# Three unused tiles among the constants of a one-layer decoder kernel

## The chip, the core and the metric

The kernel runs on one core of one Trainium2 chip. The time is device microseconds of one execution, given as the median of three runs. The trace used below is one profiled execution of the same program. Five engines matter: TensorE (PE, its weight loads are listed as PEld), VectorE (DVE), ScalarE (ACT), GpSimd (POOL) and SyncE (SP), which issues nearly all DMAs.

## The reference: what is computed

One decoder layer over 1024 tokens of width 1024, in float32. In short:

```python
h = rms_norm(x, norm_mix)
proj = h @ w_in                       # q, k, v of three mixers, and gates
oa = diff_attention(...)              # A: 4 heads, two softmaxes each
ob = banded_attention(..., 128, sink) # B: 8 heads, window 128
oc = nsa_attention(...)               # C: compressed + selected + window 512
y = einsum('nbsm,nmd->bsnd', [oa, ob, oc], w_branch)
x = x + sum(sigmoid(mg) * y) @ w_out
h = rms_norm(x, norm_mlp)
x = x + square(relu(h @ w_up)) @ w_down
```

## The kernel before

**Arithmetic.** Every float32 operand of a matrix product is split into a high and a low part by `split` (lines 87 to 91): ACT copies it to the 32-bit matmul type (the high part, line 90), and POOL or DVE subtracts that from the source (the low part, line 91). `mm3` (lines 115 to 120) then issues three matmuls into one bank of PSUM: high by high (line 118), high by low (119 or 120), low by high. In the profile a matmul reads `out<-moving,stationary`: the moving operand is streamed through the array, up to 512 columns of it, and the stationary one, 128 columns, is put in first by a weight load (PEld). A stationary slice is thus 128 float32, that is 512 bytes of each partition, and all slices of a tile lie at steps of 512 bytes.

**Stages, in order of time.** `run` (line 174) goes through them:

- Normalisation of the input into `hh` and `hl` (high and low part of the transposed, normalised input, pool `hT`), projections of mixer A and B (`project`, line 494: moving the weights, 384 or 396 columns wide, stationary `hh`/`hl`), compression, attention A and B: to 590 us.
- Mixer C, in two groups `g`: `project_c` (512 columns of weights moving, stationary `hh`/`hl`; 590 to 621 us and about 883 to 960 us), then attention C mixed on PE with `gates` (line 1095: moving `hh`/`hl`, 512 columns, stationary weights `wh`/`wl`) and, for the second group, with `first_branch` (line 1141: moving and stationary both from pool `wp`). `mix` (line 155) lays a generator of dense matmuls between the fine steps of the attention, by costs written into the code; the order on PE is the program's order, and gates are the filler that covers the attention's softmax on DVE and ACT. To 1216 us.
- `merge_and_mlp` (line 1159): the other two branch products (moving `ob` or `oc`, stationary weights that come in turn from the pools `pre` and `wx`, line 107; 1216 to 1311 us); the output projection (lines 1309 to 1318: moving `wo`, stationary `mh`/`ml`; 1311 to 1410 us).
- The MLP, as seven half-size products per pair of feature tiles, 16 pairs. Up (`up_pair`, line 1356: moving `mh`/`ml` or the sums `th`, stationary weights from `pre` and `main`; 1410 to 1736 us): each pair has 7 x 4 x 3 = 84 matmuls. Down (lines 1474 to 1519: moving weights, stationary the activations, both from `pre` and `main`; 1736 us to the end), also 84 a pair.

**Memory.** SBUF is filled from both ends by two stacks of pools. The left stack begins at byte 384 of each partition (256 bytes of DMA scratch and four constants of 32 bytes are below it). The right one ends at byte 229,344, which is 480 modulo 512. A tile's size is rounded up to 32 bytes. At the bottom of the left stack lie `cst` (`ident` 512 bytes, `nhalf` 32) and `ca` (`identr`, `gk`, `gsw`, five small ones, `cgate`, then `kct` and `vct`, 1024 bytes each). Everything else on the left begins where these two end; `ca` is released at 1216 us, so that the later pools begin where `cst` ends. From the built program, the addresses modulo 512 at which the matmul operands lie before the change ("residue" from here on; all slices of one tile share it):

| operand | pool, side | residue before |
|---|---|---|
| `hh`, `hl` | `hT`, right | 480 |
| weights, mixers A and B (396 float32 wide) | `wp`, left | 320, 384, 448, 0, 64 ... in steps of 64 |
| states of A and B | `s0`, `s1`, left | 320 |
| weights and `first_branch` operands, mixer C | `wp`, left | 192 |
| states of mixer C (base) | `sp`, left | 192 |
| `ph`, `pl` (transposed probabilities) | `at`, right | 160, and 480 in mixer C |
| `ob`; `oc` of the first half | `bb`, `br`, right | 480 |
| `oc` of the second half | `bl`, left | 416 |
| branch weights, in turn | `pre`, right; `wx`, left | 480; 416 |
| `wo` | `wo0`, `wo1`, right | 480 |
| `mh`, `ml`; `th` | `mp`, `tf`, left | 416 |
| MLP weights, activations of the down product | `pre`, `main`, right | 480 |

Of the kernel before, what the change touches and what calls it, by code (L numbers as in the profile page):

```python
# [11 lines left out]
F32 = mybir.dt.float32  # L12
# [5 lines left out]
P = 128  # L18
# [57 lines left out]
class Kernel:  # L76
# [238 lines left out]

    def idents(self):
        nc = self.nc
        self.ident = self.cst.tile([P, P], F32, name="ident")
        make_identity(nc, self.ident)
        self.identr = self.ca.tile([P, P], F32R, name="identr")  # L320
        nc.vector.tensor_copy(self.identr, self.ident)
        self.nhalf = self.cst.tile([P, 8], F32, name="nhalf")
        nc.vector.memset(self.nhalf, -0.5)
        self.gk = self.ca.tile([P, 3, HD], F32, name="gk")
        self.gsw = self.ca.tile([P, 2, HD], F32, name="gsw")

    def constants(self, tmp):
        nc, a, c = self.nc, self.a, self.ca
        ld = nc.sync.dma_start

        gains = tmp.tile([P, 8, HD], F32, name="gains")
        ld(gains, a["qk_gain"].broadcast_to([P, 8, HD]))
        stt = nc.vector.scalar_tensor_tensor
        stt(self.gk[:, 0, :], gains[:, 0, :], -0.125, gains[:, 1, :], op0=ALU.mult, op1=ALU.mult)
        stt(self.gk[:, 1, :], gains[:, 2, :], -0.125, gains[:, 3, :], op0=ALU.mult, op1=ALU.mult)
        stt(self.gk[:, 2, :], gains[:, 4, :], -0.125, gains[:, 5, :], op0=ALU.mult, op1=ALU.mult)
        stt(self.gsw[:, 0, :], gains[:, 4, :], -0.125, gains[:, 6, :], op0=ALU.mult, op1=ALU.mult)
        stt(self.gsw[:, 1, :], gains[:, 4, :], -0.125, gains[:, 7, :], op0=ALU.mult, op1=ALU.mult)

        dl = tmp.tile([P, 4, HD], F32, name="dl")  # L340
        ld(dl, a["diff_lambda"].broadcast_to([P, 4, HD]))
        pr = tmp.tile([P, 2, HD], F32, name="pr")
        nc.vector.tensor_tensor(pr, dl[:, 0:4:2, :], dl[:, 1:4:2, :], op=ALU.mult)
        ls = tmp.tile([P, 4], F32, name="ls")
        nc.vector.tensor_reduce(ls[:, 0:2], pr, axis=AX.X, op=ALU.add)
        nc.scalar.activation(ls[:, 2:4], ls[:, 0:2], AF.Exp)
        self.nlam = c.tile([P, 1], F32, name="nlam")
        stt(self.nlam, ls[:, 3:4], -LAM_INIT, ls[:, 2:3], op0=ALU.add, op1=ALU.subtract)
        self.subln = c.tile([P, 1], F32, name="subln")
        ld(self.subln, a["diff_subln"])  # L350
        nc.vector.tensor_scalar(self.subln, self.subln, 1.0 - LAM_INIT, None, op0=ALU.mult)
        self.sink = c.tile([P, 2, 8], F32, name="sink")
        ld(self.sink[:, 0, :], a["sinks"].broadcast_to([P, 8]))
        nc.vector.tensor_scalar(self.sink[:, 1, :], self.sink[:, 0, :], -1.0, None, op0=ALU.mult)
        self.wmask = c.tile([P, P], F32, name="wmask")
        ld(self.wmask, a["c_wmask"])
        self.cval = c.tile([P, 1], F32, name="cval")
        ld(self.cval, a["c_cval"])
        self.pos = c.tile([P, 2, 16], F32, name="pos")
        ld(self.pos, a["cmp_pos"])  # L360
        self.cgate = c.tile([P, NT, 24], F32, name="cgate")

        self.kct = c.tile([P, 2, P], F32R, name="kct")
        self.vct = c.tile([64, 2, P], F32R, name="vct")

# [1216 lines left out]
```

## Time and profile before

| | us |
|---|---|
| median of 3 runs | 2076.6 |
| lowest, highest | 2073.64, 2076.71 |
| span of the profiled execution | 2073.6 |

The profiled execution's span is the lowest run's time, so nothing lies around it. In the views below, a group of instructions is written as line, engine, operation, tiles, shape and count, then its busy time, the mean duration of one in ns, and the idle time before it with the engine that ended it. A view by windows gives, for each stretch of time, how long each engine was busy and (in brackets) how many of its instructions reach into the stretch, and the granted clock of TensorE as a share of full speed (PEclk).

### The profile page before, as it was taken

How to read it: one execution, taken by the hardware profiler on the slowest of the kernel's cores; microseconds unless marked ns; L12 is line 12 of the kernel's file. 1: busy time of each engine (PE TensorE's matmuls, PEld its weight loads, DVE VectorE, ACT ScalarE, POOL GpSimd, SP SyncE). 2: the span in 40 equal slices, each digit the busy share in tenths (PEclk: the TensorE clock that was granted, in tenths of full speed). 3: DMA queues.
4: the chain of work that ended last, by engine and by line, in shares of the span. 5: the costliest groups of instructions: out<-in, count | busy, mean ns of one | idle time of the engine just before them, and what ended most of it. 6: DMA issues, size and time to landing. Idle time of an engine off the chain costs nothing. (4 is left out here: it accounts for less than half of the span.)

```text
span 2073.6 us, 30616 instructions
## 1 busy us (share of the span) xinstructions
PE 1950.6 (94%) x9806; PEld 1615.6 (78%) x9806; DVE 1420.5 (69%) x3231; ACT 1019.3 (49%) x2626; POOL 948.4 (46%) x1137
## 2 busy tenths in 40 slices
PE   7999998998899999999999899999899998999998
PEld 7777777788688788787888677787688886888876
DVE  6757677788838767648676745657755444889898
ACT  5456555566636555536555533325445544434331
POOL 4555345354252212152221327217444444789784
PEclk9999999999999999999999899999999999999998
DMA  6131012011201111202142556425544346345343
GB/s 216 50 102 52 3 55 58 14 50 37 85 24 64 54 53 50 71 30 93 61 151 64 168 180 208 153 89 159 173 163 155 138 143 249 121 158 168 122 142 112
DMA packets 122557, 219.47 MB, mean 106 GB/s; under 512 B 14420, under 2 KB 35412, under 8 KB 122396
## 3 DMA queue, kind: packets, MB, share of 16 engines
q1 hardware_dynamic: 120812, 211.75, 31.3%
q10 hardware_dynamic: 1584, 5.77, 0.8%
q8 instruction: 77, 1.26, 0.3%
q14 instruction: 84, 0.69, 0.1%
HBM read 156.59 MB, written 64.81 MB: 107 GB/s over the span
## 5 line engine op out<-in xcount | busy, mean ns | idle before, releaser
L91 POOL TENSOR_TENSOR wl<-wr,wh 128x512 fp32r<-128x512 f32 (+3 forms) x246 | 326.1, 1332 | 282.1 <-ACT wh L90 236.8
L90 ACT ACTIVATE wh<-wr 128x512 fp32r<-128x512 f32 (+3 forms) x258 | 150.4, 591 | 182.3 <-PE mm L119 122.5
L705 PE MATMUL sc<-st 128*128 128x256 f32 (+5 forms) x736 | 201.6, 356 | 15.4 <-ACT p L737 15.0
L90 ACT ACTIVATE ph<-tr 128x384 fp32r<-128x384 f32 (+3 forms) x280 | 138.3, 496 | 118.0 <-PE tr L753 97.1
L91 DVE TENSOR_TENSOR pl<-tr,ph 128x384 fp32r<-128x384 f32 (+3 forms) x280 | 155.3, 558 | 45.7 <-ACT ph L90 42.4
L750 POOL MEMSET ph<- 128x128 f32 x152 | 34.7, 228 | 301.2 <-PE ac L895 256.6
L705 PEld LDWEIGHTS sc<-st 128*128 128x128 f32 x736 | 126.3, 192 | 55.7 <-ACT p L737 23.4
L118 PE MATMUL mm<-hh,wh 128*128 128x512 f32 x384 | 160.0, 417 | 0.0
L120 PE MATMUL mm<-hh,wl 128*128 128x512 f32 x384 | 152.5, 397 | 0.0
L119 PE MATMUL mm<-hl,wh 128*128 128x512 f32 x384 | 152.4, 397 | 0.0
L119 PE MATMUL mm<-wl,wh 128*128 128x512 f32 x352 | 140.4, 399 | 9.4 <-POOL wl L91 9.4
L118 PE MATMUL mm<-wh 128*128 128x512 f32 x352 | 140.5, 399 | 8.3 <-DVE x L1464 5.4
L753 PE MATMUL tr<-ident,p 128*128 128x128 f32 x792 | 132.3, 280 | 15.4 <-ACT o L883 7.9
L90 ACT ACTIVATE wh<-u 128x512 fp32r<-128x512 f32 x162 | 93.1, 620 | 107.8 <-PE mm L119 28.0
L120 PE MATMUL mm<-wh,wl 128*128 128x512 f32 x352 | 139.7, 397 | 0.0
L737 ACT ACTIVATE p<-sc,mc 128x256 f32<-128x256 f32 (+5 forms) x200 | 106.8, 538 | 51.0 <-DVE mc L729 48.9
L895 PE MATMUL ac<-ph,st 128*128 128x256 f32 x392 | 111.4, 302 | 17.2 <-DVE ob L902 11.3
L91 POOL TENSOR_TENSOR wl<-s,wh 128x512 fp32r<-128x512 f32 x64 | 87.8, 1379 | 82.8 <-ACT wh L90 82.8
L118 PE MATMUL mm<-wh,hh 128*128 128x384 f32 (+1 forms) x320 | 124.6, 389 | 0.0
L91 DVE TENSOR_TENSOR wl<-u,wh 128x512 fp32r<-128x512 f32 x98 | 110.4, 1128 | 4.1 <-ACT wh L90 4.1
L896 PE MATMUL ac<-pl,st 128*128 128x256 f32 x392 | 106.6, 293 | 5.8 <-DVE pl L91 5.2
L753 PEld LDWEIGHTS tr<-ident,p 128*128 128x128 f32 x792 | 92.0, 142 | 24.8 <-ACT o L883 10.5
(309 smaller groups left out, 5759.6 us busy)
## 6 DMA issues: line engine op xcount, KB each, us to landing
ud<-u SPq DMA_DIRECT2D x112, 256.0 KB, 2.1
u<-ud SPq DMA_DIRECT2D x98, 256.0 KB, 3.3
wr<-wu SPq DMA_DIRECT2D x76, 256.0 KB, 2.8
wr<-wd SPq DMA_DIRECT2D x64, 256.0 KB, 2.9
gd<-go SPq DMA_DIRECT2D x48, 256.0 KB, 2.0
g<-gd SPq DMA_DIRECT2D x48, 256.0 KB, 3.1
wr<-wg SPq DMA_DIRECT2D x40, 256.0 KB, 2.6
wr<-wbr SPq DMA_DIRECT2D x40, 256.0 KB, 3.0
```

The source lines that it names most:

```text
L90: nc.scalar.activation(hi, src, AF.Copy)
L91: (eng or nc.vector).tensor_tensor(lo, src, hi.bitcast(F32), op=ALU.subtract)
L118: mm(out, lh, rh, start=first, stop=False, skip_group_check=more)
L119: mm(out, lh, rl, start=False, stop=False, skip_group_check=more)
L120: mm(out, ll, rh, start=False, stop=last, skip_group_check=more)
L705: self.nc.tensor.matmul(ps[:, off:off + k1 - k0], q[:, t * P:(t + 1) * P], k[:, k0:k1], start=i == 0, stop=i == 1)
L737: self.nc.scalar.activation(p, ps, AF.Exp, bias=m, scale=-1.0, accum_out=l)
L750: nc.gpsimd.memset(ph[0:rows, o:o + P].bitcast(F32), 0.0)
L753: nc.tensor.transpose(pt[0:rows, o:o + P], src, self.ident)
L895: nc.tensor.matmul(ac, v, ph, start=first, stop=False)
L896: nc.tensor.matmul(ac, v, pl, start=False, stop=last)
```

## The change

Three tiles that nothing reads or writes are allocated between the constants: 96 bytes ahead of `ident`, 480 bytes behind `nhalf`, and 224 bytes ahead of `kct`. No instruction is added, removed or altered.

```diff
     def idents(self):
         nc = self.nc
+        self.cst.tile([P, 24], F32, name="gap0")
         self.ident = self.cst.tile([P, P], F32, name="ident")
...
         nc.vector.memset(self.nhalf, -0.5)
+        self.cst.tile([P, 120], F32, name="gap1")
         self.gk = self.ca.tile([P, 3, HD], F32, name="gk")
...
         self.cgate = c.tile([P, NT, 24], F32, name="cgate")
 
+        c.tile([P, 56], F32, name="gap2")
         self.kct = c.tile([P, 2, P], F32R, name="kct")
```

The first moves `ident` from 384 to 480. The first two together move the end of `cst` by 576 bytes, from 928 (416 modulo 512) to 1504 (480 modulo 512). All three move the end of `ca` by 800 bytes, from 192 to 480 modulo 512. So the weights and states of mixer C, `kct`, `vct`, the second half's `oc`, `wx`, `mh`, `ml` and `th` come to residue 480; the states of A and B come to 96, and the 396-wide weights to 96, 160, 224, 288, 352, 416, 480, 32. The right stack stays where it is, all of it that is named in the table at 480 but the A and B probabilities.

## The prediction

> **What bounds the kernel now.** I read the page first: the span and the share of each engine.
>
> ```profile
> span 2073.6 us, 30616 instructions
> ...
> PE 1950.6 (94%) x9806; PEld 1615.6 (78%) x9806; DVE 1420.5 (69%) x3231; ACT 1019.3 (49%) x2626; POOL 948.4 (46%) x1137
> ```
>
> PE is busy for all but 123 us. An average hides stages, so next comes the view by windows, cut at the stages' borders.
>
> ```profile
> 590.00:621.00 31.00, 31.00 (x159) 25.07 (x158) 14.71 (x26) 10.63 (x32) 21.57 (x31) 1.00 0.03 9
> 621.00:920.00 299.00, 289.44 (x1614) 242.98 (x1613) 201.37 (x642) 163.90 (x470) 77.48 (x144) 1.00 0.17 55
> 960.00:1216.00 256.00, 235.99 (x1290) 199.27 (x1288) 180.98 (x556) 139.87 (x387) 57.12 (x108) 0.95 0.31 98
> 1216.00:1311.00 95.00, 89.92 (x382) 72.72 (x383) 51.17 (x62) 29.03 (x50) 56.92 (x41) 0.98 0.70 227
> 1311.00:1410.00 99.00, 96.86 (x444) 79.52 (x443) 51.42 (x73) 27.31 (x51) 15.96 (x14) 0.98 0.31 111
> 1410.00:1736.00 326.00, 317.04 (x1354) 254.66 (x1353) 184.79 (x223) 163.23 (x276) 164.81 (x119) 0.99 0.46 157
> 1736.00:2073.00 337.00, 316.09 (x1345) 256.04 (x1343) 281.39 (x357) 127.70 (x231) 258.44 (x173) 0.97 0.47 155
> ```
>
> The columns are the stretch and its length, then PE, PEld, DVE, ACT, POOL, the granted clock, the DMA share and GB/s. In every stage PE is the fullest engine. Up and down (the last two rows) have the same number of matmuls of the same shape, yet PE is busy 317.04 and 316.09 us although the down stage contains waits. So I looked at two stretches without a gap, one in each.
>
> ```profile
> 1490.00:1740.00 250.00, 250.00 (x1074) 201.50 (x1073) 123.12 (x165) 125.13 (x207) 110.66 (x84) 1.00 0.44 153
> 1826.00:1982.00 156.00, 156.00 (x690) 129.23 (x689) 133.92 (x173) 63.13 (x114) 134.06 (x91) 1.00 0.47 153
> ```
>
> Both run at full clock with PE never idle. Records that only reach into a stretch count too, some 1.7 of them, so the matmuls start 250/1072.3 = 233.1 ns apart in up and 156/688.3 = 226.6 ns apart in down. The same 512 columns cost **6.5 ns more** in one than in the other. What differs is the residue: in up the moving operand lies at 416 and the stationary one at 480; in down both lie at 480. The mean durations, grouped by line, say the same without that correction. Up (window 1490 to 1735), then down (1826 to 1982):
>
> ```profile
> L119 PE MATMUL mm<-ml,wh 128*128 128x512 f32 x203 | 80.3, 396 | 0.0
> L118 PE MATMUL mm<-t,wh 128*128 128x512 f32 x148 | 58.5, 396 | 0.0
> ```
>
> ```profile
> L119 PE MATMUL mm<-wl,wh 128*128 128x512 f32 x182 | 70.8, 389 | 0.0
> L118 PE MATMUL tr<-wh 128*128 128x512 f32 x48 | 18.7, 389 | 0.0
> ```
>
> Is it the residue, or the stage? Four other places answer: the second projection of mixer C (883 to 902 us, moving 192, stationary 480), the gates of mixer C (621 to 920 us, moving 480, stationary 192), the first branch product of the merge (1222 to 1253 us, moving 480, stationary by turns 480 and 416) and the output projection (1339 to 1349 us, moving 480, stationary 416).
>
> ```profile
> L119 PE MATMUL sc<-wl,hh 128*128 128x512 f32 x16 | 6.3, 395 | 0.0
> ```
>
> ```profile
> L120 PE MATMUL mm<-hh,wl 128*128 128x512 f32 x192 | 75.8, 395 | 0.0
> L119 PE MATMUL mm<-hl,wh 128*128 128x512 f32 x192 | 75.7, 394 | 0.0
> ```
>
> ```profile
> L119 PE MATMUL mm<-ob,wh 128*128 128x512 f32 x46 | 18.0, 391 | 0.0
> L118 PE MATMUL mm<-ob,wh 128*128 128x512 f32 x46 | 18.0, 390 | 0.0
> L120 PE MATMUL mm<-ob,wl 128*128 128x512 f32 x46 | 17.9, 389 | 0.0
> ```
>
> ```profile
> L118 PE MATMUL mm<-wo,mh 128*128 128x512 f32 x16 | 6.4, 399 | 0.0
> L120 PE MATMUL mm<-wo,ml 128*128 128x512 f32 x15 | 5.9, 392 | 0.0
> L119 PE MATMUL mm<-wo,mh 128*128 128x512 f32 x15 | 5.8, 389 | 0.0
> ```
>
> Unequal residues give 394 to 396, the mixed group 389 to 391, equal ones 389; a stationary operand 64 bytes below the moving one (the last group) lies between, with line 118 lifted by other things ahead of it. No group with equal residues is slow. So a 512-column matmul seems to cost about 6.6 ns less when both operands start at the same address modulo 512: 396 - 389, with the starts' 6.5.
>
> **The change part by part.** No engine gets or loses an instruction, and no semaphore's owner changes; what moves is where the left stack's tiles lie. Each stage's saving is its number of 512-column matmuls that become equal, times the difference of its own rows, less what is handed to a wait.
>
> *Up.* 16 pairs x 84 = 1344 matmuls x 6.6 = 8.9 us. Not all of it lasts: early in the stage PE waits once for DVE.
>
> ```profile
> PE mm L118 <- DVE u L1381: 7.8, 1, 7.8
> ```
>
> That DVE work follows the normalisation and not PE, so what the matmuls ahead of it save only lengthens this wait: 40 us of matmuls (1410 to 1450) at 233 ns, 172 x 6.6 = 1.1 us. Behind it POOL and ACT follow PE (window 1480 to 1735 or 1760 of the waits):
>
> ```profile
> POOL wl L91 <- ACT wh L90: 148.1, 85, 15.5
> ```
>
> ```profile
> ACT wh L90 <- PE mm L119: 82.5, 63, 2.2
> ```
>
> POOL waits for ACT, which waits for PE to free buffers, so both come earlier as PE does, and the start of the down stage moves with them. Up: **7.8 us**.
>
> *Projection of mixer C.* 2 groups x 8 tiles x 8 x 3 = 384 matmuls, PE full (31.00 of 31.00): x 6.6 = **2.5 us**.
>
> *Gates in mixer C.* 20 features x 2 halves x 8 x 3 = 960 matmuls x (394.5 - 389 = 5.5) = 5.3 us. These are filler: where PE next waits for the softmax, a shorter filler makes a longer wait, and the gain is nil. In 621 to 920 us the waits are few and short:
>
> ```profile
> PE ac L895 <- DVE ob L902: 4.2, 5, 1.0
> PE sc L705 <- ACT p L737: 2.1, 4, 1.0
> PE ac L896 <- DVE pl L91: 2.1, 7, 0.5
> ```
>
> 17 waits with the one not shown, against 4 heads x 23 = 92 steps of attention in that group: many steps have slack. I take three fifths, **3.2 us**, of ends 0 and 5.3. *First branch* is at 192 on both sides and stays equal.
>
> *Merge.* The mixed groups mean 390.3 against 389, so 1.3 x 288 = 0.4, and of the second half's 96 one half goes from unequal to equal, 48 x 6.6 = 0.3; **0.7 us**.
>
> *Output projection.* 384 matmuls; its two undisturbed rows lie 3 and 0 above 389, the third less than 10. I take 2.5 each: **1.0 us** of 0 to 1.6.
>
> *The rest.* Of the 288 wide matmuls of the first gates and the compression, an eighth meets residue 480: 36 x 6.6 = **0.2 us**. The 384- and 396-column projections (1152, an eighth) I cost at nothing, at most 144 x 6.6 = 1.0. The 256-column products of probabilities by values become equal in mixer C (some 608): no clean row tells, nothing, at most half of 6.6 each, 2.0. Some 640 transposes get `ident` and their data both at 480, which no row of before shows: nothing, between -1.1 and 1.1 if it goes by columns (128 of 512). DVE, ACT and POOL read the moved tiles too; rows of DVE with a tile at 416 (`x`) and at 480 (`e`), down and up, differ by 2 ns:
>
> ```profile
> L1464 DVE TENSOR_TENSOR x<-x,mm 128x512 f32<-128x512 f32 x84 | 56.4, 679 | 11.9 <-PE mm L120 10.6 <-DMA v<-ud 0.7
> ```
>
> ```profile
> L1381 DVE TENSOR_TENSOR u<-mm,e 128x512 f32<-128x512 f32 x12 | 8.1, 677 | 0.4 <-issue 0.4
> ```
>
> so I cost them at nothing. The down stage has equal residues already, and its DVE adds to `x`, which end the kernel, follow PE.
>
> **Sum:** 7.8 + 2.5 + 3.2 + 0.7 + 1.0 + 0.2 = **15.4 us**, 2073.6 - 15.4 = 2058.2 for the profiled execution. The median of the runs lies 3.0 above that execution, which was the fastest of three: 2076.6 - 15.4 = **2061.2 us**.
>
> **The rivals.**
>
> *No effect.* The Trainium skill, "SBUF — State Buffer", section "Who interferes with whom", gives TensorE two independent read ports, one for the moving operand and one for weight loads, and says that "PE and ACT never wait on anyone". By that rule the address of one operand cannot matter to the other, and the time would stay 2076.6. The trace disagrees, 396 against 389 ns. As a mechanism of this kernel: the 6.6 ns belong to the stage or the pool, not to the residue. For it: no tile of this trace is seen at two residues. Against it: unequal rows occur in four stages, with moving operand on either side, and `ob` in one short window mixes both. Or the tiles end elsewhere than I added up; same result. 2076.6 us.
>
> *Absorbed.* PE's gain in the up stage and in the gates comes back as waits, and only the projection, the merge and the output remain: 2.5 + 0.7 + 1.0 = 4.2, or 2072.4. For it: DVE waits 1.1 us longer at the head, as said. Against it: the rows of POOL and ACT that wait for PE, and no idle PE in 1490 to 1740.
>
> *Slower, by the granted clock.* Long waits of PE are followed by a lower clock: the stretch around the 7.8 us wait, and that at the start of down, have
>
> ```profile
> 1445.00:1465.00 20.00, 12.23 (x45) 9.46 (x44) 15.32 (x14) 6.30 (x11) 13.07 (x8) 0.83 0.45 146
> 1740.00:1760.00 20.00, 12.91 (x42) 9.22 (x41) 7.14 (x9) 9.33 (x17) 15.10 (x11) 0.74 1.02 386
> ```
>
> With less filler, waits in attention C grow; if they grow enough, the clock falls there too. The second group already has 0.95, the first 1.00. If both lost another 0.05 of 299 + 256 us, that is 27.8 us, against 12.2 left without the gates: 2092. It decides where a wait passes from at most 1.0 us (621 to 920) to about 3, the longest in the second group:
>
> ```profile
> PE sc L705 <- ACT p L737: 10.5, 9, 3.1
> ```
>
> A step's filler loses some 24 x 5.5 = 0.13 us, far from that.
>
> **How the numbers follow.** Forecast 0.80, no effect 0.08, absorbed 0.08, slower 0.04. The forecast's own bounds: with nothing from the gates and the output and 1.1 lost to transposes, 10.1 us or 2066.5; with everything, 8.9 + 2.5 + 5.3 + 0.7 + 1.6 + 0.2 + 1.0 + 2.0 + 1.1 = 23.3, 2053.3. Executions scatter by 1.5 us to either side of the middle of 2073.64 and 2076.71. Range **2052 to 2068**. A measurement of this kernel tells about 0.2% (4 us) from no change: faster 0.86 (the forecast and most of "absorbed"), same 0.10, slower 0.04.
>
> **What would show it.** Right: in up, the gates and the projection of mixer C, mean durations of 389 where 394 to 396 stood; up from its DVE wait to the start of down shorter by 7.8; down, attention A and B unchanged. The filler step is wrong if the waits of 621 to 1216 us grow by over 5. The whole is wrong if those durations stay at 395.

## The result, and the profile after

| | before | after |
|---|---|---|
| median of 4 runs | 2075.12 us | 2061.18 us |
| lowest, highest | 2072.13, 2076.71 us | 2058.76, 2065.39 us |
| ratio of times, 95% interval | | 0.993 [0.9912, 0.9948] |
| span of the profiled execution | 2073.6 us | 2058.2 us |

Later comparisons gave 2061.53 against 2073.77 (0.9937 [0.9918, 0.9957]) and 2059.29 against 2073.09 (0.993 [0.9913, 0.9947]). So the change is worth 12 to 14 us, and 2061.2 had been forecast. The instructions are the same on every engine, and so is the order in which each works through them; the page of the changed kernel begins:

```profile
span 2058.2 us, 30616 instructions
...
PE 1926.9 (94%) x9806; PEld 1607.2 (78%) x9806; DVE 1419.3 (69%) x3231; ACT 1017.9 (49%) x2626; POOL 951.5 (46%) x1137
```

PE's busy time went from 1950.6 to 1926.9 us, 23.7 less, while the span lost 15.4; that of the other engines moved by at most 3.1 (weight loads, which go with PE, by 8.4). The 8.3 us between 23.7 and 15.4 are more idle time of PE, spread over the stages (2.5 of them before 590 us). Lines behind the gaps now have numbers up to 3 higher (L1381 is L1384). The view by windows, in a part of up without a gap (columns as in the prediction):

```profile
1490.00:1700.00 210.00, 210.00 (x928) 173.83 (x928) 106.31 (x144) 108.01 (x179) 102.28 (x76) 1.00 0.45 155
```

With the 1.7 records that only reach into it, 210/926.3 = 226.7 ns from start to start, where before had 233.1. The groups of matmuls in up (window 1490 to 1720):

```profile
L119 PE MATMUL mm<-ml,wh 128*128 128x512 f32 x194 | 75.5, 389 | 0.0
L118 PE MATMUL mm<-t,wh 128*128 128x512 f32 x144 | 56.0, 389 | 0.0
```

Both were 396. Next come the second projection of mixer C (883 to 900 us), then the first one (592 to 620 us), where transposes on line 555 break the row of matmuls (a row is a run of 512-column matmuls with nothing else of PE between them):

```profile
L119 PE MATMUL sc<-wl,hh 128*128 128x512 f32 x14 | 5.4, 389 | 0.0
```

```profile
L119 PE MATMUL sc<-wl,hh 128*128 128x512 f32 x18 | 7.0, 391 | 0.0
L120 PE MATMUL sc<-wh,hl 128*128 128x512 f32 x18 | 7.1, 392 | 0.0
```

Both were 395, but only the unbroken one came to 389. The gates in mixer C (621 to 860 us) stop short of it too:

```profile
L119 PE MATMUL mm<-hl,wh 128*128 128x512 f32 x181 | 70.9, 392 | 0.0
L120 PE MATMUL mm<-hh,wl 128*128 128x512 f32 x181 | 70.9, 392 | 0.0
```

And the merge's first product (1223 to 1253 us) and the output projection (1339 to 1349 us):

```profile
L120 PE MATMUL mm<-ob,wl 128*128 128x512 f32 x44 | 17.1, 389 | 0.0
L118 PE MATMUL mm<-ob,wh 128*128 128x512 f32 x43 | 16.7, 389 | 0.0
```

```profile
L118 PE MATMUL mm<-wo,mh 128*128 128x512 f32 x14 | 5.5, 395 | 0.0
L120 PE MATMUL mm<-wo,ml 128*128 128x512 f32 x14 | 5.5, 390 | 0.0
```

What part of it was handed on to waits? PE's waits at the head of up (1402 to 1740 us), in the merge (1208 to 1304; before's row stands ahead of it), and in the two groups of mixer C (960 to 1208, then 621 to 919): engine, line and what it waited for, then us in total, times, the longest.

```profile
PE mm L118 <- DVE u L1384: 8.9, 1, 8.9
```

```profile
PE mm L118 <- DVE g L1201: 4.1, 2, 3.1
```

```profile
PE mm L118 <- DVE g L1204: 5.2, 2, 4.5
```

```profile
PE sc L708 <- ACT p L740: 11.3, 9, 3.1
```

```profile
PE ac L898 <- DVE ob L905: 4.3, 5, 1.0
PE ac L899 <- DVE pl L91: 2.4, 8, 0.5
PE sc L708 <- ACT p L740: 2.2, 5, 1.0
```

The first was 7.8, so it grew by 1.1, and so did the merge's. The second group's was 10.5, with the same longest, 3.1. The last three were 8.4 in sum and are 8.9.

### The profile page after: what moved, and what is told of

Its sections match the earlier page's. It is cut to its first block, busy times and chain, and to the rows that moved or that the text cites. A ratio compares the mean times of both kernels' runs of the same rounds, so it can differ in the third digit from the quotient of the medians.

```text
span 2058.2 us, 30616 instructions
## 1 busy us (share of the span) xinstructions
PE 1926.9 (94%) x9806; PEld 1607.2 (78%) x9806; DVE 1419.3 (69%) x3231; ACT 1017.9 (49%) x2626; POOL 951.5 (46%) x1137
## 5 line engine op out<-in xcount | busy, mean ns | idle before, releaser
L91 POOL TENSOR_TENSOR wl<-wr,wh 128x512 fp32r<-128x512 f32 (+3 forms) x246 | 327.7, 1339 | 276.4 <-ACT wh L90 232.6
L898 PE MATMUL ac<-ph,st 128*128 128x256 f32 x392 | 110.0, 299 | 17.0 <-DVE ob L905 11.3
```

Of the source, the lines that this page charges most:

```text
L91: (eng or nc.vector).tensor_tensor(lo, src, hi.bitcast(F32), op=ALU.subtract)
L898: nc.tensor.matmul(ac, v, ph, start=first, stop=False)
```

## The experiments

The theory: a 512-column matmul is some 6.6 ns cheaper when its moving and its stationary operand start at the same address modulo 512, whatever that address is. The rivals: an address of its own that is good or bad, the stage or pool rather than the address, waits that take the gain back, and a clock that happened to be higher in the profiled execution.

### PE alone, one distance after the other (e1_micro)

A kernel of its own, with the whole layer left out: 24 groups of 40 back-to-back matmuls, in which only the start of the moving operand and, in the last nine groups, the width change. Beside PE only a copy of each finished group runs.

```python
CASES = [(512, o) for o in (16, 0, 1, 2, 4, 8, 16, 32, 48, 64, 96, 112, 120, 127, 0)]
CASES += [(384, o) for o in (0, 16, 64)] + [(256, o) for o in (0, 16, 64)] + [(128, o) for o in (0, 16, 64)]
...
            for r in range(REP):
                k = r % 4
                nc.tensor.matmul(z[:, 0:n], sta[:, k * P:(k + 1) * P], mov[:, o:o + n],
                                 start=r == 0, stop=r == REP - 1)
```

> A kernel of its own that leaves the whole layer out: runs of 40 matmuls into one PSUM tile each, the stationary slices at steps of 512 bytes, the moving operand starting 0, 4, 8, 16, 32, 64, 128, 192, 256, 384, 448, 480 or 508 bytes behind them modulo 512; 512 columns, then 384, 256 and 128 columns at 0, 64 and 256 bytes. No other engine works beside PE. Theory (equal start modulo 512 is the fast case): about 226.7 ns from start to start (mean duration 389) at 0, 229 to 233.3 (392 to 396) at every multiple of 32 that is not 0. Open: offsets below 32 bytes, and narrower matmuls, where the layer kernel's rows show at most 1 to 2 ns. Rival 'load of the other engines': with PE alone all offsets give the same. Rival 'stage or pool': the same, since all cases use the same two tiles.

Groups of matmuls; the name of the output tells the case: `zb` starts equal, `zc` 4, `zg` 64, `zh` 128, `zj` 256 and `zl` 448 bytes apart; `zs` and `zt` have 256 columns, 0 and 64 bytes apart.

```profile
L41 PE MATMUL zb<-mov,sta 128*128 128x512 f32 x40 | 9.2, 389 | 0.0
L41 PE MATMUL zc<-mov,sta 128*128 128x512 f32 x40 | 9.6, 398 | 0.0
L41 PE MATMUL zg<-mov,sta 128*128 128x512 f32 x40 | 9.3, 391 | 0.0
L41 PE MATMUL zh<-mov,sta 128*128 128x512 f32 x40 | 9.4, 394 | 0.0
L41 PE MATMUL zj<-mov,sta 128*128 128x512 f32 x40 | 9.2, 389 | 0.0
L41 PE MATMUL zl<-mov,sta 128*128 128x512 f32 x40 | 9.5, 395 | 0.0
L41 PE MATMUL zs<-mov,sta 128*128 128x256 f32 x40 | 5.0, 283 | 0.0
L41 PE MATMUL zt<-mov,sta 128*128 128x256 f32 x40 | 4.9, 279 | 0.0
```

From start to start, once settled (mean of the last 20); the distance is how far the moving operand starts behind the stationary one, modulo 512:

| bytes apart | 0 | 4 | 8 | 16 | 32 | 64 | 128 | 192 | 256 | 384 | 448 | 480 | 508 |
|---|---|---|---|---|---|---|---|---|---|---|---|---|---|
| 512 columns, ns | 226.7 | 236.7 | 233.2 | 231.7 | 233.3 | 229.1 | 232.6 | 233.3 | 226.7 | 233.3 | 233.3 | 233.3 | 226.7 |

384 columns take 173.3 at 0, 64 and 256; 256 columns 120.0 at 0 and 256 and 117.8 at 64; 128 columns 111.7 throughout. So the effect needs no other work and no other stage. Of the four widths it belongs to 512 columns, and its period is **256 bytes**, not 512. Why the chip does this, no run shows. It isn't there at once either. The first start-to-start times (ns) of `zj` and of `zh`, read from the trace:

```text
zj (256 bytes apart): 226 236 228 233 231 226 227 227 226 227 227 226 227
zh (128 bytes apart): 229 231 233 231 229 230 232 241 232 231 232 228 230
```

The groups at 0, 256 and 508 bytes take two to six steps to settle at 226.7; the others never do in their 40 matmuls.

### Half the change at a time (e2_tail_only, e3_c_only)

The expectations below speak of stretches at half clock. In these traces the granted clock is either 1.0 or 0.5, and the 0.5 comes in stretches of mostly 3.4, 6.8 or 10.2 us: 16 of them, some 72 us, in before's profiled execution.

Without the third gap, merge, output and up become equal (480 on both sides) and mixer C doesn't:

```diff
+        self.cst.tile([P, 24], F32, name="gap0")
         self.ident = self.cst.tile([P, P], F32, name="ident")
...
+        self.cst.tile([P, 120], F32, name="gap1")
```

> Gaps 0 and 1 without gap 2: mh, ml, th, wx and the second half's oc come to 480, but weights and states of mixer C to 256. Theory: up, merge and output projection at 389 ns a matmul, 9.5 us less than before (about 2065.6, ratio 0.995); the projection and gates of mixer C stay at 394 to 396. Rival 'clock': most of the gain came from fewer stretches at half clock in the second attention group, which have nothing to do with the tail; then this kernel gains at most 3 us with durations of 389 in up all the same.

One gap of 288 bytes ahead of `kct` instead of the three makes mixer C alone equal:

```diff
+        c.tile([P, 72], F32, name="gap2")
         self.kct = c.tile([P, 2, P], F32R, name="kct")
```

> One gap of 288 bytes ahead of kct and no other: weights and states of mixer C come to 480, mh, ml, th and wx stay at 416. Theory: projection of mixer C at 389, its gates at about 392 (their runs are too short to settle), up at 395 to 396: 2 to 5 us less than before (2070 to 2073, ratio 0.9985 to 0.999). Rival 'clock': the stretches at half clock in the second attention group go with the shifted filler, and this kernel gains 8 us or more.

Groups in up (1500 to 1700 us) and in the second projection of mixer C (885 to 900 us), of the tail alone, then of mixer C alone:

```profile
L119 PE MATMUL mm<-t,wh 128*128 128x512 f32 x126 | 49.0, 389 | 0.0
...
L120 PE MATMUL sc<-wh,hl 128*128 128x512 f32 x11 | 4.3, 395 | 0.0
```

```profile
L119 PE MATMUL mm<-t,wh 128*128 128x512 f32 x124 | 48.9, 394 | 0.0
...
L119 PE MATMUL sc<-wl,hh 128*128 128x512 f32 x11 | 4.3, 389 | 0.0
```

Each goes to 389 exactly where its starts are equal. The ends of matmuls are modelled in these profiles, their starts are not: from start to start, up (1500 to 1700 us) has 226.7 ns in the tail alone and 233.3 in mixer C alone, as before, so the 394 there is no gain. The tail alone took 2064.12 us, 0.996 [0.9946, 0.9974]; mixer C alone 2070.5, 0.9986 [0.9971, 1.0001]; before, in the same comparison, had 2073.07. That is 9.0 and 2.6 us less. The 9.0 agrees with the forecast's terms for up, merge and output (7.8 + 0.7 + 1.0 = 9.5). The 2.6 is less than half of those for mixer C (2.5 + 3.2 = 5.7), though its interval, 0 to 6 us, reaches that far. Together they make 11.6 us, close to the 12 to 14 of the whole change, and the rival that put most of it down to the clock gave the tail 3 us at most.

### The same shift, 64 bytes too far (e4_plus64)

```diff
-        self.cst.tile([P, 120], F32, name="gap1")
+        self.cst.tile([P, 136], F32, name="gap1")
```

> The change with gap 1 larger by 64 bytes, so that everything it brought to 480 lies at 32, and the right stack at 480. Theory (the distance counts, by the rows of before): up has the stationary operand 64 below the moving one, about 229 ns from start to start (392); output projection and gates have it 64 above, 233 (395 to 396); projection of mixer C 229. 8 to 9 us slower than the changed kernel, about 2069, ratio to before 0.997. Rival 'the gaps as such' (other waits between old and new tiles, not the residue): as fast as the changed kernel, 2061.

Groups in up (1500 to 1700 us), left at 32 and right at 480:

```profile
L118 PE MATMUL mm<-mh,wh 128*128 128x512 f32 x168 | 66.2, 394 | 0.0
L120 PE MATMUL mm<-mh,wl 128*128 128x512 f32 x168 | 65.9, 392 | 0.0
L119 PE MATMUL mm<-ml,wh 128*128 128x512 f32 x168 | 65.2, 388 | 0.0
```

Their mean is 391.3, between equal (389) and the 396 of before. The direction counts: before, the moving operand lay 64 bytes ahead of the stationary one (416 and 480), which is 448 in the table of PE alone (233.3); here it lies 64 bytes behind (229.1). From start to start up has 228.9 ns here. The time lies between as well: 2067.72 us, 0.9986 [0.9975, 0.9998]. The medians differ by 5.4 us, while the ratio amounts to 2.9, so the size is known to a few us only; in the profiled executions up alone is 4.4 us shorter than before's. In up the distance decides, and not the gaps as such, by which this kernel would have been as fast as the changed one.

### The other stack moved instead (e7_right64)

A pool of 64 bytes at the bottom of the right stack takes its tiles from 480 to 416, and the left one stays as it was:

```diff
+        rg = tc.alloc_tile_pool(name="rg", bufs=1, side="right")
+        rg.tile([P, 16], F32, name="gapr")
...
+        rg.release()
```

> The kernel before with one gap of 64 bytes at the top of the right stack and none at the left: hh, hl, pre, main, wo and ob go to 416, where mh, ml, th and wx already are; weights and states of mixer C stay at 192. Theory 'only the distance counts': up, merge and output projection at 389, projection and gates of mixer C at 394 to 396, time as with gaps 0 and 1 alone (ratio 0.996). Rival 'the address itself counts' (480 is a good place, or any change of the left stack's overlaps): 395 in up, ratio 1.000.

Groups in up and in the second projection of mixer C, which is unequal in this kernel too:

```profile
L119 PE MATMUL mm<-ml,wh 128*128 128x512 f32 x169 | 65.7, 389 | 0.0
...
L119 PE MATMUL sc<-wl,hh 128*128 128x512 f32 x11 | 4.3, 395 | 0.0
```

2063.57 us, 0.995 [0.9932, 0.9968]. Up is as quick with both sides at 416 as with both at 480. So neither address is a good one by itself, and no tile of the left stack had to move.

### 256 bytes apart, twice (e5_mod256, e9_mod256_again), and the change again (e6_after_again, e10_after_third)

The first of these puts the left stack at 224, 256 bytes from the right one; the second is the same kernel again, timed next to the changed one.

```diff
-        self.cst.tile([P, 120], F32, name="gap1")
+        self.cst.tile([P, 56], F32, name="gap1")
```

> The change with gap 1 smaller by 256 bytes: what it brought to 480 lies at 224, the right stack at 480. Theory after the run of matmuls alone, where an offset of 256 bytes was as fast as none: the period is 256 and not 512, so 389 ns in up and a time like the changed kernel's, 11 to 12 us under before (ratio 0.9945). Rival 'modulo 512', as the change's name has it: 395 in up, as before (ratio 0.999 to 1.001).

> The changed kernel once more, with more executions. Theory 'residue alone': what its two parts gave separately adds up, 9.0 (gaps 0 and 1) + 2.6 (one gap ahead of kct) = 11.6 us, ratio 0.9944; the other 4 us of the profiled pair came from 12 us less at half clock in that execution and do not come back. Rival 'the clock belongs to the change': 14 to 15 us, ratio 0.993.

> The kernel with everything at 224 once more, on one chip with the next two. Theory 'the half-clock stretches': its 4.7 us lead over the changed kernel came from the run of executions (its profile shows no half-clock stretch before 1161 us, the others three or four there); both then lie within 2 us of each other, ratio to before 0.993 to 0.995. Rival 'an offset of 256 is better than none': 0.9925 or less, and again 4 us under the changed kernel.

> The changed kernel beside it: ratio to before 0.993 to 0.995, 11 to 14 us, by both theories.

A group in up, 256 bytes apart:

```profile
L118 PE MATMUL mm<-mh,wh 128*128 128x512 f32 x168 | 65.4, 389 | 0.0
```

So 256 bytes count as equal in the layer too: 0.9928 [0.9905, 0.9951] and 0.9939 [0.9916, 0.9961], the changed kernel beside them 0.9937 and 0.993. In the first pair the shorter shift led by 4.7 us (2056.85), in the second it was behind by 2.8 (2062.07). That is scatter, and the profiles show of what kind. The span and mean granted clock of the first, then of the second:

```profile
core 0: 2052.9 us, clock 0.987
```

```profile
core 0: 2066.4 us, clock 0.982
```

The same kernel differs by 13.5 us between two executions; 0.005 of 2060 us is 10.3 of them, if PE is at work in that time. Over all 13 executions this kernel has a mean of 2060.5 us, the changed one 2060.4 over its 16.

The change again had been expected at 11.6 us if only the distance counts, and at 14 to 15 if the higher clock of the profiled execution belongs to the change. Its two comparisons, 12.2 and 13.8 us, don't tell these apart, but the clocks of all executions do: before's 53 executions in the comparisons have a mean granted clock of 0.984 (0.980 to 0.988) and a mean time of 2073.4 us, the changed kernel's 16 the same 0.984 (0.982 to 0.987) and 2060.4. So the change doesn't raise the clock, and 13.0 us are gained at an equal one. From one execution of before to another, 0.001 of the clock goes with some 1.5 us.

### How long a row must be (e8_short_runs)

The gates do not reach 389. Of their 219 rows in mixer C, in the trace of the changed kernel, 163 are only 3 long, and PE alone needed up to six. The kernel has nothing of the layer: rows of 3, 6, 12 or 24 matmuls with equal starts or 128 bytes apart, and four matmuls each of 256 and 128 columns behind every row.

```python
CASES = [(24, 0)] + [(run, o) for run in (3, 6, 12, 24) for o in (0, 32)]
...
            for _ in range(48 // n):
                seq += [(512, o)] * n + [(256, 0)] * 4 + [(128, 0)] * 4
```

> A kernel of its own that leaves the layer out: runs of 3, 6, 12 and 24 matmuls of 512 columns, broken by four of 256 and four of 128 columns, each with the moving operand starting 0 or 128 bytes behind the stationary one; 48 wide matmuls a case. Theory 'it settles' (an equal start lets the spacing fall to 226.7 ns after some six matmuls, a break undoes it): at distance 0, 392 to 393 in runs of 3, 391 in runs of 6, 390 in runs of 12, 389 to 390 in runs of 24; at 128 bytes 394 to 395 in all. Rival 'the gates of mixer C stay slow because of the other engines': 389 at distance 0 in runs of any length.

Groups of matmuls: `zb` and `zc` are rows of 3, `zh` and `zi` rows of 24, the first of each equal, the second 128 bytes apart.

```profile
L42 PE MATMUL zb<-mov,sta 128*128 128x512 f32 x48 | 14.6, 411 | 0.0
L42 PE MATMUL zc<-mov,sta 128*128 128x512 f32 x48 | 14.6, 412 | 0.0
L42 PE MATMUL zh<-mov,sta 128*128 128x512 f32 x48 | 11.4, 392 | 0.0
L42 PE MATMUL zi<-mov,sta 128*128 128x512 f32 x48 | 11.6, 397 | 0.0
```

Rows of 6 gave 400 and 403, rows of 12 gave 396 and 399. The difference is 1, 3, 3 and 5 ns: it grows with the length, as the settling says, and no other engine works beside these rows that could hold the short ones back. The absolute numbers missed what was expected, because the first matmul of each row is recorded some 280 ns ahead of the next and with a duration of some 446 ns, whatever the addresses, and a row of 3 divides that by 3. Little of it is lost time: the first of the narrowest matmuls is only some 59 ns ahead of the next, where 111.7 is their step, so part of it is a shift of the starts where the width changes. A whole round, a row of 3 with its eight narrow matmuls, takes 1620 ns equal and 1626 at 128 bytes, where the settled steps of PE alone add up to 1607. A round with a row of 24 takes 6393 and 6508. So an equal start is worth 2.1 ns a matmul in rows of 3 and 4.8 in rows of 24.

### The gates in longer rows (e11_long_gates)

The change, with the gates of mixer C given out in rows of 12 matmuls where they came by threes; amount and total cost of the filler stay:

```diff
-                    yield 0.65
+                    if self.w_n < 512:
+                        yield 0.65
+                    elif k % 4 == 3:
+                        yield 2.6
```

> The changed kernel, with the gates of mixer C handed out in runs of 12 matmuls instead of 3; the same work, in another order on PE. Theory 'an equal start needs some six matmuls to settle': the gates' lines 119 and 120 in 621 to 860 us fall from about 392 to 390 or 391, 960 x 1.5 to 2 = 1.4 to 2 us of PE time. What the coarser filler does to the attention's waits is open: with few waits there (10 us in the first group) 0 to 4 us more of them, so the time lies within 3 us of the changed kernel. Rival 'load of the other engines': the gates stay at 392.

2095.34 us, 1.0108 [1.0084, 1.0131]: some 34 us slower than the changed kernel, where a time within 3 us of it had been expected. The gates themselves (621 to 838 us) did get a little cheaper, as the settling has it; if the other engines held them back, they would have stayed at 392:

```profile
L120 PE MATMUL mm<-hh,wl 128*128 128x512 f32 x159 | 62.1, 391 | 0.0
L119 PE MATMUL mm<-hl,wh 128*128 128x512 f32 x159 | 62.0, 390 | 0.0
```

The same two lines of the changed kernel have 392 in this window. But the first group now reaches to 940 us. The window of that stretch in this kernel, and further down its waits on DVE from 621 to 919 us:

```profile
621.00:940.00 319.00, 294.12 (x1618) 248.19 (x1617) 200.69 (x642) 163.47 (x465) 75.91 (x147) 0.98 0.16 50
```

The same stretch of the changed kernel:

```profile
621.00:940.00 319.00, 309.13 (x1727) 261.08 (x1725) 216.72 (x685) 175.21 (x503) 93.37 (x164) 1.00 0.18 55
```

Back to the long rows, the waits:

```profile
PE ac L898 <- DVE ob L905: 13.7, 8, 2.5
PE ac L899 <- DVE pl L91: 5.8, 13, 1.2
```

PE is idle for 24.9 of the 319 us, against 9.9, and the granted clock is 0.98 instead of 1.00. The two waits were 4.3 and 2.4 us. All six executions have a lower mean clock, 0.978 to 0.981, than those of the changed kernel (0.982 to 0.987). The second group, whose filler has gates too, loses as well: from the end of its projection to the merge it takes 294.6 us, against 278.6, and the first group, from its first gate to the second projection, 282.0 against 261.4. A filler piece of 12 matmuls is 2.7 us in which no step of the attention can start; that DVE is late for this reason is my reading of the rows, and no run took it apart from the other things that move with it.

## Why the prediction came out as it did

**The mechanism was right.** Rows with equal starts went to 389 ns, those with the moving operand 64 bytes behind lay between, and no other part of the change is needed for that (e1, e2, e3, e4, e7). The rule of the Trainium skill that was weighed, "SBUF — State Buffer", section "Who interferes with whom", has two independent read ports in TensorE; on PE alone 226.7 became 233.3 ns by moving one operand 32 bytes, so as far as the address goes the two are not independent. The rivals "no effect" (2076.6), "absorbed" (2072.4) and "slower" (2092) all fell. What was off is the modulus, 256 bytes in place of 512, and the sizes of some terms.

The table gives each stage's share of the difference to before's profile, from the starts of the same matmuls in both traces (us). All columns compare with the one profile of before, whose own luck is in each of them.

| stage, by before's times | forecast | change | change, again | change, third | tail alone | C alone |
|---|---|---|---|---|---|---|
| 0 to 590 | -0.2 | +1.3 | +3.0 | +1.1 | +1.0 | +0.3 |
| 590 to 960 | -4.1 | -1.4 | -2.8 | -2.1 | +0.2 | -2.2 |
| 960 to 1216 | -1.6 | -8.0 | -8.5 | -4.6 | -3.2 | -0.8 |
| merge, to 1311 | -0.7 | +0.9 | +2.3 | +2.6 | +0.9 | +1.9 |
| output, to 1410 | -1.0 | -1.0 | -0.4 | -2.8 | -2.4 | -3.2 |
| up: head, to 1458 | 0 | 0.0 | -0.1 | 0.0 | 0.0 | 0.0 |
| up: rest, to 1760 | -7.8 | -7.4 | -7.5 | -6.5 | -7.6 | +0.9 |
| down | 0 | +0.2 | -0.3 | -2.3 | -0.3 | +0.3 |
| sum | -15.4 | -15.4 | -14.3 | -14.6 | -11.3 | -2.8 |

(The forecast's gates, 3.2, are shared evenly between the two groups, and its rest, 0.2, stands in the first row. Rounding leaves 0.1 in some sums.)

- **Up, 7.8: right.** The four executions of the table with equal starts in up have 6.5 to 7.6. What the head saves does go into the wait on DVE (7.8 to 8.9 us), the 1.1 that was taken off.
- **Output, 1.0: of the right size by its rows**, 399 to 395 and 392 to 390 with the third line unchanged at 389, or some 2 ns of 384 matmuls, 0.8 us. The stage itself scatters by more: mixer C alone, which leaves it as it was, has -3.2.
- **Merge, 0.7: the rate was right, the gain wasn't kept.** The rows went to 389, but the stage did not become shorter in any of the three; in the profiled pair PE's wait on DVE `g` grew by 1.1 us, more than the 0.7, which the sum had not allowed for. The stage scatters as well: mixer C alone has +1.9.
- **Projection of mixer C, 2.5: too much.** The full 6.6 was given to all 384 matmuls. In the first group transposes break the row, and it stands at 391 to 392. The second group's projection (from 883 us) went from 48.0 to 47.3 us in each of the three executions of the change, 0.8 for the 1.25 of its half.
- **Gates, 3.2: the rate was wrong, and the discount stood for something that hardly shows.** 394 to 395 became 392, not 389, so 960 of them have 960 x 2.5 = 2.4 us to give at most. The rate in the sum came from long rows, while the gates come by threes. The three fifths were meant for slack before the softmax, but the three waits in 621 to 919 us only went from 8.4 to 8.9 us in sum, and in 960 to 1216 us PE's idle time changed by +1.3, -1.5 and +0.6 us in the three executions. Stages 590 to 960 show what the projection and the rate had too much: -1.4 to -2.8 for -4.1.
- **The terms put at nothing held where a row shows them.** 384 columns take 173.3 ns at any of the three distances (e1). In 621 to 838 us the 256-column products had 284 ns and have 284 and 285, the transposes 276 and 276.
- **960 to 1216 us: not foreseen.** The profiled pair has -8.0 here for the 1.6 forecast. This makes up for the terms that were too large, and so the profiled pair's sum agrees to the decimal by luck. The row of this stage (960 to 1208 us) in six executions: before, the changed kernel, the same again, the same a third time, the tail alone, and 64 bytes too far:

```profile
960.00:1208.00 248.00, 229.16 (x1249) 193.41 (x1248) 177.24 (x550) 136.78 (x381) 56.07 (x102) 0.96 0.31 100
```

```profile
960.00:1208.00 248.00, 226.62 (x1289) 192.40 (x1287) 180.34 (x556) 139.80 (x387) 57.96 (x108) 0.99 0.32 102
```

```profile
960.00:1208.00 248.00, 229.17 (x1291) 195.07 (x1289) 178.64 (x557) 139.86 (x387) 57.26 (x108) 0.98 0.31 102
```

```profile
960.00:1208.00 248.00, 228.22 (x1277) 194.58 (x1276) 178.34 (x553) 138.78 (x385) 58.06 (x108) 0.97 0.31 100
```

```profile
960.00:1208.00 248.00, 229.27 (x1264) 194.22 (x1263) 178.70 (x555) 138.25 (x384) 56.44 (x103) 0.97 0.32 102
```

```profile
960.00:1208.00 248.00, 226.72 (x1286) 191.60 (x1285) 180.10 (x556) 139.30 (x386) 56.94 (x108) 0.99 0.31 101
```

Read the granted clock, third from the right; before's execution had 0.96, and 0.01 of 248 us is 2.5 us. The changed kernel has 0.99, 0.98 and 0.97 in its three. At 0.97 it stands at -4.6, and the tail alone, whose mixer C is not equal, at -3.2. At 0.99 it has -8.0, and the kernel 64 bytes off -6.7. At the same clock some 1.3 to 1.4 us are left to the change, near the 1.6 of the forecast; most of the rest goes with the clock. The execution at 0.98 doesn't fit: it has -8.5, more than its clock explains. Why an execution gets more or less clock in this stage, the runs don't settle; over whole executions the change doesn't raise it (a mean of 0.984 with it and without it).

- **Bridge from span to time: wrong in one place.** Before's span was taken for its lowest run's time. In the changed kernel's runs the time is 1.8 to 2.0 us above the span (2060.2 and 2058.2 for the profiled one), so before's profiled execution is estimated at some 2075.5, though none of the four measured times is that. The subtraction from the median, 2076.6 - 15.4, was not touched by that, but that median of three was itself 2.8 to 3.5 above before's later ones (2073.07 to 2073.77). In the three comparisons 15.4 is 1.5 to 3.2 us more than was gained, about what the terms for 590 to 960 us had too much (1.3 to 2.7). In the first comparison the high median and the high sum cancel, so that 2061.18 came out for 2061.2 is luck too; that it lies in the range is not.

The best of the versions tried is the change itself, with the 256-byte one beside it; none beats it by more than the scatter.

## What to carry to other kernels

Where PE is full and its matmuls are 512 columns wide, compare the start-to-start time of long rows between stages: if equal shapes differ by 2 to 3%, look at the distance of the two operands modulo 256 bytes, and mend it with a gap in either stack. This is shown for 32-bit operands, 512 columns and a new weight slice for every matmul, and for nothing else. Count the gain only for rows long enough to settle, and take the rate for short rows from short rows. Two profiles that agree with a forecast to the decimal prove little where one stage of one kernel scatters by several us with the clock: halves of the change and repeated runs say which term was right.

## What was not expected of the hardware

- The distance of the operands is graded: 4 bytes cost 10.0 ns a matmul (236.7 against 226.7), 64 bytes 2.4, most others 5 to 6.6, 256 none, and 508 none either, though that is only 4 bytes in the other direction. 256 columns go the other way, 120.0 equal against 117.8 at 64 bytes, and 384 and 128 columns don't care.
- The gain comes after two to six matmuls in a row, and some seven behind narrower matmuls. Such a break looks dearer than it is: the second matmul of a row starts some 280 ns after the first, but a whole round with a row of 3 takes only 13 ns more than its settled steps.
- The Trainium skill, "TensorE: Matmul & The Clock Gate", section "Wait — 56ns, not 53.3ns?", gives 215.7 ns from start to start at 512 columns. The lowest here, with these 32-bit operands and a weight load for every matmul, is 226.7, on PE alone and in the layer.
- Four times longer filler pieces cost 34 us, and the whole change to the addresses brought 12 to 14: in this kernel the length of PE's filler pieces outweighs a few ns on each matmul.
